# Three accumulator banks in a new order, and gate rows and key stores on GpSimd's queue

## The chip, the cores and the metric

The kernel runs on one core of one Trainium2 chip. The metric is device time in microseconds (us) of one execution, smaller is better; times of before are those of 3 runs. A traced execution has its own time, and a span: the stretch from its first to its last traced instruction.

## The reference, cut to what matters

One layer of a diffusion backbone over 512 latent tokens with 256 context tokens in front, width 2048, all in float32. Six modulation vectors come out of a gemv of the condition `c` with `w_ada`. Both token sets are normed and modulated and go through one input projection, which is split into the queries, keys and values of 8 differential heads and the low-rank parts of 8 latent heads.

```python
mod_x = silu(c) @ w_ada[l] + b_ada[l]               # 6 vectors of 2048: shift, scale, gate, twice
p = modulate(rmsnorm(x), sh1, s1) @ w_in            # and the same for the context tokens
q_da, k_da, v_da = heads(p[..., :3072])             # 8 heads of 128 each, rotary on q and k
c_q, c_kv = rmsnorm(p[..., 3072:3456]), rmsnorm(p[..., 3456:3712])
k_rope = p[..., 3712:]
w = softmax(q1 @ k1.T * s) - lam * softmax(q2 @ k2.T * s)   # differential heads: two maps a head
o_da = w @ v_da                                      # then latent heads, merge, output projection
x = x + g2 * ((silu(conv(g)) * u) @ w_down)          # gated MLP, then a final norm
```

## The kernel before, in words

Every float32 operand is split in two (`split`, L245: ScalarE casts the high part, VectorE subtracts for the low part), and a product is three matmuls (`mm3`, L281) of some 0.23 us each for 512 columns.

**Stages.** The profile's time axis has these: up to about 140 us the norm, the first modulation rows and the first five features; from 140 to 296 us the *feature stage*; from 296 to 425 us the *values*; then attention, the output projection and the MLP.

**The feature stage** (L863 to L885) makes the remaining key features of the differential heads (f = 0 to 5), the rotary key (f = 6) and three features `cq` for the latent queries. Each feature takes two weight blocks of 512 KB. A block is loaded by `wload` (L257, SP's queue, a ring of three `wr` tiles), cast by ScalarE to `wh` (L248, L268 for the rotary one) and completed by VectorE with `wl` (L249). A finished key feature goes through `keys` (L759): rotary, split into `kh` and `kl`, and `put` (L768) stores both to DRAM, 384 KB each. After each feature come `next_gemv` calls (L875, L885): three rows for f = 0 to 5, two for the others, 26 in all. One row is a load of 1024 KB into a ring of two `ada` tiles (L349) and one VectorE instruction (L352, "gate row" from here on) that leaves one column of modulation in `modx`. All of these loads and stores are issued on SP's queue, which takes them one after the other: an issue that waits (for a ring's tile, or for `kl`) holds all issues behind it. Only the three `cq` pairs are stored through GpSimd's queue. The order of the instructions in this stage is not written by hand, the framework's scheduler lays it out from the program and a model of times.

**The values** (L902 to L945) multiply all 768 tokens by the value weights in two halves of 512 columns. Each half has six accumulators, one for each 128 tokens: four lie in the two `s` tiles and two in banks of the ring `b`. After a half, its six accumulators leave PSUM by a split into `v` tiles (L248, L249), which GpSimd's queue stores (L945). The second half leaves in the order 2, 3, 4, 5, 0, 1: first the four in the `s` tiles, then the two in banks of `b`. The last splits write tiles whose earlier content must first have been stored.

**PSUM.** Four of the eight banks are the ring `b` (pool `ps_b`), handed out in turn by `b_tile` (L242). Up to the values 19 tiles have been taken from it: 8 in the first stage, one for each of 7 features, 3 for `cq`, one for a sum. So the first half of the values takes banks 3 and 0 (counted from 0), the second half banks 1 and 2. Then the pool is released (L949) and `ps_a` takes the same four banks in the order in which its tags are first asked for, L1071 to L1073: `po` (sums of weighted values), `f` (query features), two of `pt` (transposed weights). A new tile waits for the instructions that read the old tile of its bank.

**Attention's start.** The steps of attention are put into one order by the list scheduler `Flow.run` with times of its own, which doesn't know banks. TensorE's first work is the query feature of head 1 (`da_feature`, L1130) into `f`: 7 steps of three matmuls, then the first scores of head 0 (L1013) into an `s` tile, then feature steps and scores in turn. VectorE takes the row maxima of the scores (L1016), ScalarE the exponentials (L1018). `pt` and `po` come into use with the weighted values of head 0, some 40 us after attention's start.

Of the kernel before, what the change touches and what calls it, by code (L numbers as in the profile page):

```python
# [109 lines left out]
class Flow:  # L110
# [7 lines left out]
    def buf(self, make, ring=None, count=None):  # L118
        if ring:
            self.rings[ring] = count  # L120
        return Buf(ring, make)
# [99 lines left out]
def layer_kernel(ctx: ExitStack, tc: tile.TileContext, small, rope, c_row, cc_row, x_t, ctx_t, ada, ada_k,  # L221
                 w_g0, w_f, w_v, w_uqn, w_uqr, w_ukv, w_o, w_up0, w_up, w_dn, out_t):
    nc = tc.nc
    pe, ve, sc, gp = nc.tensor, nc.vector, nc.scalar, nc.gpsimd
# [8 lines left out]
    def nm(s):  # L233
        n[0] += 1
        return f"{s}{n[0]}"
# [6 lines left out]
    def b_tile(tag="b", bufs=None):  # L242
        return ps_b.tile([P, 512], F32, tag=tag, name=nm(tag), bufs=bufs or nb[0])

    def split(dst_h, dst_l, src, scale=None):  # L245

        if scale is None:
            sc.copy(dst_h, src)  # L248
            ve.tensor_tensor(dst_l, src, dst_h.bitcast(F32), op=ALU.subtract)  # L249
        else:  # L250
            sc.mul(dst_h, src, scale)
            ve.scalar_tensor_tensor(out=dst_l, in0=src, scalar=scale, in1=dst_h.bitcast(F32),
                                    op0=ALU.mult, op1=ALU.subtract)
# [19 lines left out]
    def wblock(src):  # L273
        return wsplit(wload(src))
# [25 lines left out]
    def col(name, j=0):  # L300
        o = OFF[name] + j
        return smt[:, o:o + 1]
# [8 lines left out]
    modx = cst.tile([P, 96], F32, name="modx")  # L311
# [26 lines left out]
    def rstd(out, ssq, dim, t1, t2):  # L338

        sc.activation(out, ssq, AF.Ln, bias=epst, scale=1.0 / dim)  # L340
        sc.activation(out, out, AF.Exp, scale=-0.5)
        ve.tensor_scalar(out=t1, in0=ssq, scalar1=1.0 / dim, scalar2=EPS, op0=ALU.mult, op1=ALU.add)
        ve.scalar_tensor_tensor(out=t2, in0=out, scalar=-0.5, in1=out, op0=ALU.mult, op1=ALU.mult)
        ve.tensor_tensor(t2, t2, t1, op=ALU.mult)
        ve.scalar_tensor_tensor(out=out, in0=t2, scalar=1.5, in1=out, op0=ALU.add, op1=ALU.mult)

    def gemv(pool, j, srcs, bufs=2):
        w = pool.tile([P, D], F32, tag="ada", name=nm("ada"), bufs=bufs)
        nc.sync.dma_start(w, ada[j])  # L349
        for i, (vec, dst) in enumerate(srcs):  # L350
            junk = w if i == len(srcs) - 1 else pool.tile([P, D], BF16, tag="junk", name=nm("junk"), bufs=1)
            ve.tensor_tensor_reduce(out=junk, in0=w, in1=vec, op0=ALU.mult, op1=ALU.add, scale=1.0,  # L352
                                    scalar=col("b_ada", j), accum_out=dst[:, j:j + 1])
# [10 lines left out]
    cb = st.tile([P, D], F32, name="cb")  # L364
# [83 lines left out]
    for p in range(8):  # L448
# [5 lines left out]
        def ctx_square(q=q, kts=kts, p=p):  # L454
            if p in ON_DVE:
                ve.tensor_tensor(hv(q(), kts, 1), cv(kts), cv(kts), op=ALU.mult)
            else:
# [3 lines left out]
             w=[q], hold=[cr[p // 2]])  # L461
# [34 lines left out]
    for k, (c0, c1) in enumerate(((0, T), (T, TT))):  # L496
        r, s, g = rinv[:, c0:c1], slice(c0, c1), 1 - 0.38 * k
# [233 lines left out]
    kv = tc.alloc_tile_pool(name="kv", bufs=1, reuse_waits="tile")  # L731
    kvs = tc.alloc_tile_pool(name="kvs", bufs=2, reuse_waits="tile")
    cb = kv.tile([P, D], F32, name="cb1")
# [7 lines left out]
    def next_gemv(pool, count):  # L741
        for _ in range(count):
            j = next(gv, None)
            if j is not None:
                gemv(pool, j, [(cb, modx)])

    lo, hi = slice(0, 64), slice(64, 128)

# [16 lines left out]
        split(kh[:, T:], kl[:, T:], co)  # L765
        put(dst, (kh, kl))

    def put(dst, hl, queue=nc.sync):  # L768
        for i in range(2):
            queue.dma_start(dst[i], hl[i].bitcast(F32))  # L770

# [6 lines left out]
                                    op0=ALU.mult, op1=ALU.subtract)  # L778
        return qs

    def latent_norm(tiles, squares, s, width, dim, wname, dst, queue=nc.sync):
        total = squares[0][:, :width]
        root = []

        def add():
            for q in squares[1:]:
                ve.tensor_tensor(total, total, q[:, :width], op=ALU.add)
            for c0, c1 in [(0, T)] if width == T else [(0, T), (T, width)]:
                pe.matmul(s[:, c0:c1], ones32, total[:, c0:c1], start=True, stop=True)

        def roots():
            r, t1, t2 = (kv.tile([P, TT], F32, tag=g, name=nm(g), bufs=1)[:, :width] for g in ("nr", "n1", "nq"))
            rstd(r, s[:, :width], dim, t1, t2)
            root.append(r)

        def scaled(i, t):
            ve.scalar_tensor_tensor(out=t, in0=t, scalar=col(wname, i), in1=root[0], op0=ALU.mult, op1=ALU.mult)
            hl = [kvs.tile([P, TT], F32R, tag=g, name=nm(g))[:, :width] for g in ("kh", "kl")]
            split(hl[0], hl[1], t)
            put(dst[i], hl, queue)  # L800

        return [add, roots] + [lambda i=i, t=t: scaled(i, t) for i, t in enumerate(tiles)]
# [60 lines left out]
    for f in range(7):  # L863
        lat, co = b_tile(), s_tile()[:, :T]
        if f < 6:
            feature(lat, co)
            keys(k_d[f + 2], lat, halves_sum(co))
            if f == 0:
                for part in latent_norm(ckv, sq, s_tile(), TT, KVR, "kvn", ckv_d):
                    part()  # L870
        else:
            rotary_feature(lat, co)
            lat = parts_sum(lat, kv.tile([P, T], F32, tag="qs0", name=nm("lt"), bufs=1))
            keys(kr_d, lat, parts_sum(halves_sum(co), kv.tile([P, C], F32, tag="ct", name=nm("ct"), bufs=2)))
        next_gemv(kv, 3 if f < 6 else 2)  # L875
    cq, sq = [], []
    for i in range(3):
        lat = b_tile()
        feature(lat, None)
        sq.append(kv.tile([P, TT], F32, tag=("nq", "nr", "n1")[i], name=nm("nq"), bufs=1))  # L880
        sc.square(sq[i][:, :T], lat)
        t = kv.tile([P, TT], F32, tag="lt", name=nm("cq"), bufs=3)[:, :T]
        sc.copy(t, lat)
        cq.append(t)
        next_gemv(kv, 2)  # L885
    queries = latent_norm(cq, sq, b_tile(), T, QR, "qn", cq_d, gp)
    raws, rows = [], []

# [35 lines left out]
    with tc.manual_schedule(engines={mybir.EngineType.PE, mybir.EngineType.Activation, mybir.EngineType.DVE,  # L924
# [4 lines left out]
        for half in range(2):  # L929
# [8 lines left out]
            for t in order:  # L938
                hl = []
                for _ in range(2):  # L940
                    pool, g, bufs = homes.pop(0)
# [27 lines left out]
    def block(t, *src):  # L969

        cols = sum(p.shape[1] for p in src)
        raw = fetch(t, src, cols)
        hi = buf(lambda: wp.tile([P, 1024], F32R, tag="wh", name=nm("wh"), bufs=3), "wh", 3)
        lo = buf(lambda: wp.tile([P, 1024], F32R, tag="wl", name=nm("wl"), bufs=3), "wl", 3)
        step("ACT", 0.05 + cols * 0.00088, t - 4, lambda: sc.copy(hi()[:, :cols], raw()[:, :cols]), r=[raw], w=[hi])
        step("DVE", 0.02 + cols * 0.0011, t - 2.8, lambda: ve.tensor_tensor(
            lo()[:, :cols], raw()[:, :cols], hi()[:, :cols].bitcast(F32), op=ALU.subtract), r=[raw, hi], w=[lo],
             lock=True)
        return hi, lo
# [76 lines left out]
    def weights_tile():  # L1056
        return buf(lambda: dp.tile([P, TT], F32, tag="p0", name=nm("p0"), bufs=8), "p0", 8)
# [10 lines left out]
    da.tile([P, T], F32, tag="rt", name=nm("rt"), bufs=2)  # L1068
    for _ in range(4):
        weights_tile().make()  # L1070
    b_tile("po", 1)  # L1071
    b_tile("f", 1)
    b_tile("pt", 2)  # L1073
    zeroed = [buf(lambda t=t: t) for t in klz]
    for n_, (t, b) in enumerate(zip(klz, zeroed)):
        for i, r in enumerate((hi, lo)):
# [75 lines left out]
    for h in range(NH):  # L1152
# [21 lines left out]
        if h + 1 < NH:  # L1174
# [4 lines left out]
            else:  # L1179
# [3 lines left out]
        hl = wvals[h]  # L1183
        flow.part = f"w{h}"
        weighted_values(BASE[h + 1] + 4.0, 3.05, ws, lambda kt, hl=hl: [g()[:, kt * P:(kt + 1) * P] for g in hl],
                        lambda kt, hl=hl: hl, o,
                        lambda t, o, h=h: step("SP", 0.4, t, lambda: nc.sync.dma_start(o_d[h], o()), r=[o],
                                               w=[o_ready[h]]))
# [63 lines left out]
    def head_value(t, p, kt, w, s=None):  # L1252

        out = s or buf(lambda: b_tile("f", 1), "f", 1)
        o = TT if s else 0

        def mm():
            for j in range(2):
                mm3(out()[:, o:o + 256], [g[:, kt * P:(kt + 1) * P] for g in lat["ckv"][j]],
                    [g()[:, j * 256:j * 256 + 256] for g in w], j == 0 and not s, j == 1, s is not None)  # L1260

        if kt % 3 == 0:
            mv[p, kt // 3] = [vals(g) for g in ("vh", "vl")]
        c = slice(kt % 3 * 256, kt % 3 * 256 + 256)
        step("PE", 0.73, t, mm, r=[*w, latent_open], w=[out])
        parts(t + 0.95, mv[p, kt // 3], out, lambda b: b()[:, c], lambda: out()[:, o:o + 256], None, 0.27, 0.4)
# [55 lines left out]
    for h in range(-1, NH):  # L1322
# [19 lines left out]
        for qt in range(NQT):  # L1342
# [8 lines left out]
            if i == 0 and qt == 3:  # L1351
# [4 lines left out]
                   None if kt is None else lambda t, s, kt=kt: head_value(t, p, kt, vw[p], s))  # L1356
# [37 lines left out]
    def a2k(dt=F32, pool=None):  # L1394
        return (pool or pools["apa"]).tile([P, 512], dt, tag="a2k", name=nm("a2k"))
# [14 lines left out]
    for kb in range(8):  # L1410
        t = tw + 8 * 0.9 * kb
        w = block(t, w_o[0, kb])
        for j in range(2):
            h = 2 * kb + j
            hl = [buf(lambda: a2k(F32R)), buf(lambda: a2k(F32R, pools["apb"]))]
# [29 lines left out]
    cb = wo.tile([P, D], F32, name="cb2")  # L1445
# [34 lines left out]
    for g in range(3):  # L1480
# [7 lines left out]
        for kb in range(8 if g else 0):  # L1488
            next_gemv(wo, 1)
            w = g1_first.pop(0) if g1_first else wblock(w_o[g, kb])  # L1490
# [138 lines left out]
    queue = []  # L1629
# [569 lines left out]
```

## Time and profile before

| | |
|---|---|
| median of 3 runs | 2345.67 us (2344.15 to 2346.49) |
| the traced execution | 2343.4 us |
| its span | 2341.6 us |
| granted TensorE clock, mean | 0.993 |
| busy in the span: TensorE, VectorE, ScalarE, GpSimd | 98%, 74%, 50%, 11% |

The rows of stages give the busy time of PE, PEld, DVE, ACT and POOL in that order, each with its count of instructions. Busy time of TensorE counts matmuls whose ends are modelled, so 98% says that it rarely stands still and not that each matmul runs at its best pace. A granted clock of 1.00 is 2.4 GHz. In the rows, L is a line of the kernel, "PEld" is TensorE's weight load, "SPq" and "POOLq" are the DMA issues of SyncE's and GpSimd's queues, and an arrow in brackets gives the idle time of the engine before the instruction and what ended it.

### The profile page before, as it was taken

What the parts mean: (1) busy time and instruction counts of PE and PEld (TensorE: products, weight loads), DVE (VectorE), ACT (ScalarE), POOL (GpSimd) and SP (SyncE); (2) the same over time, 40 slices, a digit from 0 to 9 for tenths busy, and PEclk for the clock granted to TensorE, in tenths of its full rate; (3) what the DMA queues carried; (4) which work ended last, traced back from release to release, by engine and by line L of the source; (5) the groups of instructions that cost most, each with busy time, mean ns of one, the idle gap of its engine ahead of it and who ended that gap; (6) DMA issues with size and microseconds to landing.
All of it is one profiled execution on the core that took longest, in us unless ns stands there. A gap on an engine that the chain in (4) does not pass through costs nothing.

```text
span 2341.6 us, 32200 instructions
## 1 busy us (share of the span) xinstructions
PE 2292.9 (98%) x12378; PEld 1960.5 (84%) x12378; DVE 1729.7 (74%) x2206; ACT 1166.3 (50%) x1777; POOL 267.7 (11%) x308
## 2 busy tenths in 40 slices
PE   6999999999999999999999999999999999999998
PEld 5788788788888888898888888888888888888887
DVE  7988876598987676597685858585858585767667
ACT  6541311477767522355454545454545454545456
POOL 0000001100123212000101010101010101010110
PEclk8999999999999999999999999999999999999999
DMA  9978989545311197234647374646464555555563
GB/s 370 368 254 293 354 321 324 176 123 164 126 35 41 55 349 279 100 102 142 144 117 165 105 172 115 159 121 153 126 145 134 137 143 144 131 149 126 154 184 105
DMA packets 124731, 404.23 MB, mean 173 GB/s; under 512 B 14337, under 2 KB 18945, under 8 KB 114081
## 3 DMA queue, kind: packets, MB, share of 16 engines
q1 hardware_dynamic: 96658, 346.92, 44.3%
q0 software_dynamic: 26768, 54.21, 12.5%
q8 instruction: 97, 1.59, 0.3%
q10 hardware_dynamic: 1152, 1.05, 0.1%
q14 instruction: 56, 0.46, 0.1%
HBM read 332.45 MB, written 69.67 MB: 172 GB/s over the span
## 4 chain that ended last, share of the span: by engine, by line
PE 84%; DVE 7%; issue 4%; DMA 3%; ACT 1%; POOL 0%; SPq 0%; DVEq 0%; ACTq 0%; POOLq 0%
PE y L1911 13%; PE b L284 9%; PE b L285 9%; PE b L286 9%; PE y L1913 7%; PE z L1911 6%; PE s L1013 4%; PE z L1913 3%; PE x L1911 3%; PE s L284 3%; PE s L285 3%; PE s L286 3%; DMA ada<-in_ada 2%; PE x L1913 2%; PE f L284 2%
## 5 line engine op out<-in xcount | busy, mean ns | idle before, releaser
L1735 DVE TENSOR_TENSOR wl<-wr,wh 128x1024 fp32r<-128x1024 f32 x144 | 176.4, 1225 | 158.9 <-ACT wh L1727 158.2
L1932 POOL DMA_DIRECT2D x_d<-xs x160 | 139.7, 1000 | 1147.5 <-ACT xs L1931 1145.6
L1727 ACT CAST wh<-wr 128x1024 fp32r<-128x1024 f32 x144 | 150.8, 1048 | 216.6 <-PE b L285 119.2
L284 PE MATMUL b<-ah,wh 128*128 128x512 f32 (+1 forms) x664 | 256.8, 387 | 0.0
L285 PE MATMUL b<-al,wh 128*128 128x512 f32 (+1 forms) x664 | 256.7, 387 | 0.0
L286 PE MATMUL b<-ah,wl 128*128 128x512 f32 (+1 forms) x664 | 255.9, 385 | 0.0
L1735 DVE TENSOR_TENSOR wl<-rb,wh 128x1024 fp32r<-128x1024 f32 x123 | 149.9, 1219 | 120.6 <-ACT wh L1727 120.6
L1735 DVE TENSOR_TENSOR wl<-ws,wh 128x1024 fp32r<-128x1024 f32 x123 | 150.3, 1222 | 110.4 <-ACT wh L1727 110.4
L1727 ACT CAST wh<-rb 128x1024 fp32r<-128x1024 f32 x123 | 129.3, 1051 | 182.7 <-PE b L285 80.1
L1911 PE MATMUL y<-a2k,wh 128*128 128x512 f32 x656 | 164.0, 392 | 0.0
L1727 ACT CAST wh<-ws 128x1024 fp32r<-128x1024 f32 x123 | 128.4, 1044 | 68.2 <-PE b L285 48.8
L286 PEld LDWEIGHTS b<-ah,wl 128*128 128x128 f32 x664 | 124.8, 188 | 25.7
L284 PEld LDWEIGHTS b<-ah,wh 128*128 128x128 f32 x664 | 125.1, 188 | 22.9
L285 PEld LDWEIGHTS b<-al,wh 128*128 128x128 f32 x664 | 125.1, 188 | 21.9
L1911 PEld LDWEIGHTS y<-a2k,wh 128*128 128x128 f32 x656 | 118.6, 189 | 21.6
L248 ACT CAST wh<-wr 128x1024 fp32r<-128x1024 f32 x51 | 53.5, 1051 | 160.6 <-DMA wr<-in_w_v 47.1
L352 DVE CUSTOM_DVE_ANT_0 ada<-ada,cb,smt 128x2048 f32<-128x2048 f32 x42 | 101.5, 2418 | 26.4 <-DMA ada<-in_ada 26.4
L1018 ACT ACTIVATE p<-s,m 128x768 f32<-128x768 f32 x96 | 86.8, 905 | 48.3 <-DVE m L1016 47.0
L1016 DVE TENSOR_REDUCE m<-s 128x1 f32<-128x768 f32 x96 | 91.0, 950 | 24.5 <-PE s L1013 24.2
L1911 PE MATMUL y<-b2k,wh 128*128 128x512 f32 x410 | 106.8, 390 | 0.0
L1931 ACT ACTIVATE xs<-b,modx 128x512 f32<-128x512 f32 x160 | 101.2, 681 | 1.7 <-DMA x_d<-xs 1.6
L1913 PEld LDWEIGHTS y<-a2k,wl 128*128 128x128 f32 x656 | 89.5, 190 | 6.4
(523 smaller groups left out, 5931.5 us busy)
## 6 DMA issues: line engine op xcount, KB each, us to landing
ada<-in_ada SPq DMA_DIRECT2D x80, 1024.0 KB, 6.8
rb<-in_w_up SPq DMA_DIRECT2D x123, 512.0 KB, 4.4
wr<-in_w_dn SPq DMA_DIRECT2D x88, 512.0 KB, 3.6
x_d<-xs POOLq DMA_DIRECT2D x160, 256.0 KB, 6.0
wr<-in_w_up SPq DMA_DIRECT2D x53, 512.0 KB, 4.2
wr<-in_w_f SPq DMA_DIRECT2D x34, 512.0 KB, 6.9
adak<-in_ada_k SPq DMA_DIRECT2D x32, 512.0 KB, 7.5
wr<-in_w_o SPq DMA_DIRECT2D x32, 512.0 KB, 6.5
```

Source lines behind the costliest of these rows:

```text
L284: pe.matmul(out, st[0], mv[0], start=start, stop=False, **kw)
L285: pe.matmul(out, st[0], mv[1], start=False, stop=False, **kw)
L286: pe.matmul(out, st[1], mv[0], start=False, stop=stop, **kw)
L352: ve.tensor_tensor_reduce(out=junk, in0=w, in1=vec, op0=ALU.mult, op1=ALU.add, scale=1.0, scalar=col("b_ada", j), accum_out=dst[:, j:j + 1])
L1013: pe.matmul(s()[:, c0:c1], a, b[:, c0:c1], start=i == 0, stop=i == len(ms) - 1)
L1016: step("DVE", 0.87, t + cost + 0.2, lambda: ve.tensor_reduce(out=m(), in_=s()[:, :TT], axis=AX.X, op=ALU.max, negate=True), r=[s], w=[m])
L1727: sc.copy(t, raw[:, k * n_:k * n_ + n_])
L1735: ve.tensor_tensor(t, raw[:, k * n_:k * n_ + n_], hi[k].bitcast(F32), op=ALU.subtract)
L1911: pe.matmul(o, w[j][0], hs[j], start=start and j == 0, stop=False, skip_group_check=True)
L1913: pe.matmul(o[:, h0], w[j][1], hs[j][:, h0], start=False, stop=j == 7, skip_group_check=True)
L1931: sc.mul(x, po, modx[:, 80 + dt:81 + dt])
L1932: gp.dma_start(x1_d[dt], x, accum_op=ALU.add)
```

## The change

Three edits. `gemv` takes a queue, and rows asked for with the pool `kv` (the 26 of the feature stage) are loaded through GpSimd's queue; the rows during the values (`load_row`, L893) and those of later stages stay on SP's. `put` and `latent_norm` have GpSimd's queue as default: that moves 24 stores of the features, 16 of keys (`k_d`), 2 of the rotary key (`kr_d`), 2 of the first queries (`q0_d`) and 4 of the latent keys and values (`ckv_d`). And attention's pool asks for `pt` first, so its banks are `pt`, `pt`, `po`, `f`.

```diff
-    def gemv(pool, j, srcs, bufs=2):
+    def gemv(pool, j, srcs, bufs=2, queue=nc.sync):
         w = pool.tile([P, D], F32, tag="ada", name=nm("ada"), bufs=bufs)
-        nc.sync.dma_start(w, ada[j])
+        queue.dma_start(w, ada[j])
...
             if j is not None:
-                gemv(pool, j, [(cb, modx)])
+                gemv(pool, j, [(cb, modx)], queue=gp if pool is kv else nc.sync)
...
-    def put(dst, hl, queue=nc.sync):
+    def put(dst, hl, queue=gp):
         for i in range(2):
             queue.dma_start(dst[i], hl[i].bitcast(F32))
...
-    def latent_norm(tiles, squares, s, width, dim, wname, dst, queue=nc.sync):
+    def latent_norm(tiles, squares, s, width, dim, wname, dst, queue=gp):
...
     for _ in range(4):
         weights_tile().make()
+    b_tile("pt", 2)
     b_tile("po", 1)
     b_tile("f", 1)
-    b_tile("pt", 2)
```

## Rows read from the trace of the kernel before

**Rows 1.** Stages: window, length, busy us of five engines, clock, DMA, GB/s.

```profile
140.00:256.00 116.00, 116.00 (x567) 98.03 (x566) 98.12 (x143) 32.12 (x49) 0.00 (x0) 1.00 0.83 296
256.00:296.00 40.00, 37.85 (x159) 30.38 (x158) 35.71 (x40) 15.49 (x23) 0.00 (x0) 0.96 0.94 349
296.00:425.00 129.00, 128.86 (x567) 106.06 (x565) 83.50 (x82) 23.47 (x29) 14.19 (x21) 1.00 0.92 320
425.00:440.00 15.00, 10.39 (x39) 8.48 (x40) 4.61 (x6) 3.60 (x6) 7.00 (x10) 0.77 0.68 258
```

**Rows 2.** TensorE's waits before and after 425 us: total, times, longest.

```profile
PE b L286 <- DVE wl L249: 2.1, 1, 2.1
...
PE f L284 <- DVE v L249: 4.7, 1, 4.7
```

**Rows 3.** TensorE in order of time where attention starts: start, us, instruction.

```profile
424.48 0.39 PE L286 MATMUL b<-wh,a4k 128*128 128x512 f32 x1
429.61 0.80 PE L284 MATMUL f<-a4k,wh 128*128 128x512 f32 x1 [4.75 <-DVE v L249]
...
433.62 0.45 PE L284 MATMUL f<-a4k,wh 128*128 128x512 f32 x1
...
436.44 0.39 PE L1013 MATMUL s<-ks,qs 128*128 128x512 f32 x1
```

**Rows 4.** VectorE in order of time at the same place.

```profile
428.87 0.69 DVE L249 TENSOR_TENSOR v<-b,n 128x512 fp32r<-128x512 f32 x1 [2.08 <-DMA v_d<-v]
431.19 0.69 DVE L249 TENSOR_TENSOR v<-b,v 128x512 fp32r<-128x512 f32 x1 [1.63 <-DMA v_d<-v]
437.32 0.96 DVE L1016 TENSOR_REDUCE m<-s 128x1 f32<-128x768 f32 x1 [5.44 <-PE s L1013]
```

**Rows 5.** TensorE in order of time at the last features' start.

```profile
256.46 0.40 PE L285 MATMUL b<-a4k,wh 128*128 128x512 f32 x1
...
258.93 0.50 PE L286 MATMUL b<-a4k,wl 128*128 128x512 f32 x1 [2.06 <-DVE wl L249]
...
262.78 0.53 PE L284 MATMUL b<-a4k,wh 128*128 128x512 f32 x1
```

**Rows 6.** VectorE in order of time before that.

```profile
224.30 2.56 DVE L249 TENSOR_TENSOR wl<-wr,wh 128x1024 fp32r<-128x1024 f32 x2
...
242.71 0.69 DVE L270 TENSOR_TENSOR wh<-wr,wh 128x512 fp32r<-128x512 f32 x1 [0.25 <-ACT wh L268]
...
251.27 2.35 DVE L352 CUSTOM_DVE_ANT_0 ada<-ada,cb,smt 128x2048 f32<-128x2048 f32 x1 [2.90 <-DMA ada<-in_ada]
...
254.79 2.33 DVE L352 CUSTOM_DVE_ANT_0 ada<-ada,cb,smt 128x2048 f32<-128x2048 f32 x1
...
257.65 1.22 DVE L249 TENSOR_TENSOR wl<-wr,wh 128x1024 fp32r<-128x1024 f32 x1
```

**Rows 7.** ScalarE at the same place.

```profile
255.02 1.05 ACT L248 CAST wh<-wr 128x1024 fp32r<-128x1024 f32 x1 [7.10 <-DMA wr<-in_w_f]
```

**Rows 8.** SP's queue in order of time, its issues with their waits inside.

```profile
224.79 8.92 SPq L349 DMA_DIRECT2D ada<-in_ada  x2
233.76 0.90 SPq L257 DMA_DIRECT2D wr<-in_w_f  x2
...
242.86 4.64 SPq L349 DMA_DIRECT2D ada<-in_ada  x2
247.56 0.91 SPq L257 DMA_DIRECT2D wr<-in_w_f  x2
```

**Rows 9.** GpSimd's queue: its first store of that stage, start and us.

```profile
322.03 0.60 POOL L770 DMA_DIRECT2D cq_d<-kh  x1 [189.26 <-ACT kh L248]
```

**Rows 10.** DMA issues of the whole span: count, KB each, median us to landing.

```profile
ada<-in_ada SPq DMA_DIRECT2D x80, 1024.0 KB, 6.8
...
q_d<-qs SPq DMA_DIRECT2D x2, 256.0 KB, 5.9
...
cq_d<-kh POOLq DMA_DIRECT2D x3, 256.0 KB, 7.1
```

## The prediction

> **What bounds the kernel now.** I read the busy times by stage first, because the page alone (TensorE busy for 98% of the span) doesn't say where TensorE stands still. In the feature stage and in the values TensorE is busy throughout and its clock is 1.00; two short stretches are different: 256 to 296 us, with 37.85 us busy of 40, and 425 to 440 us, with 10.39 of 15 and a granted clock of 0.77 [rows 1]. TensorE sets the time, then, and what the change can win lies in these two places, or is nothing. TensorE's waits say the same in one line each: 2.1 us for a `wl` of VectorE, once, and 4.7 us for a VectorE `v` split, once [rows 2]. Both waits end on VectorE, so I went on to the order of time of TensorE and VectorE there, and from VectorE to what it waited for: SP's queue.
>
> **The place at 425 us.** The last matmul of the values starts at 424.48; one takes 0.23 us, so TensorE is free at 424.71. The first matmul of `f` starts at 429.61, after a wait for VectorE [rows 3]. VectorE's split that ends just before (428.87 + 0.69 = 429.56) is the last but one of the second half; the last one runs from 431.19 to 431.88, and both waited until earlier `v` tiles were stored [rows 4]. That agrees with the count of banks: `f` is second in its pool, bank 1, which the second half's first `b` accumulator held, and that leaves fifth of six. The gap costs 429.61 - 424.71 = 4.90 us. It costs more behind it: the next nine matmuls take from 429.61 to 433.62, 4.01 us, where nine at 0.23 take 2.07 [rows 3]; that is the stretch with the lower granted clock, of which a matmul at 0.43 shows the 1.2 GHz level and one at 0.23 the 2.4 GHz level. That is 1.94 us more, 6.84 us in all.
>
> With `pt`, `pt`, `po`, `f` the tile `f` lies in bank 3. By the same count that is the first half's first `b` accumulator, which left when half of the 129 us of the values was over [rows 1], some 60 us earlier. Nothing else holds `f`: its two weight blocks are complete before the values end. So I take the gap and the slow clock away. `po` moves to bank 2, which leaves last (431.88), and `pt` to banks 0 and 1; they are wanted some 40 us later, and that time hides it.
>
> What is late next? The first scores start at 436.44 [rows 3]; they would start after 7 feature steps of three matmuls, 424.71 + 21 x 0.23 = 429.54, which is 6.90 earlier. The first row maximum started at 437.32 after VectorE had idled for 5.44 us; it can't start before the last split ends at 431.88, so it moves by 5.44 only [rows 4]. TensorE has nine feature steps more to do beside the scores, so I expect the later scores to keep most of the 6.8. Bounds 5.4 and 6.9; I take 6.6, near the upper one, since it is TensorE and not VectorE that the trace shows late there.
>
> **The place at 257 us.** Here the second part of the change counts. TensorE's matmul with `wl` starts at 258.93 where 256.46 + 0.23 = 256.69 was due: 2.24 us. Then ten matmul starts take from 258.93 to 262.78, 3.85 us for 2.30: 1.55 us of lower clock [rows 5]. Together 3.8 us. The `wl` ran at 257.65 behind two gate rows, of which the first had waited 2.90 us for its `ada` load [rows 6]; its `wh` was cast at 255.02 after 7.10 us of waiting for the weight load [rows 7]. Both loads came late from SP's queue. A pair of `ada` issues occupies it for 8.92 us (the second waits until a gate row gives its tile back) and the pair of weight loads behind comes at 233.76; the same again, 4.64 us, and weights at 247.56 [rows 8]. The tiles for these weights were free once VectorE had done with them: at 224.30 + 2.56 = 226.86 for the first pair and at 242.71 + 0.69 = 243.40 for the second [rows 6]. On their own queue the weights could go 6.9 and 4.2 us earlier.
>
> For the stall to go, the `wl` must move from 257.65 to 255.4, by 2.2 us. If VectorE keeps its order, it has to get both gate rows done earlier, and the first can move by its 2.90 us of waiting at most. It would, if its load weren't slowed: 1 MB of weights that now goes in the middle of the `ada` loads takes 3.5 us at the stage's 296 GB/s [rows 1] and would have gone before. The margin is 0.7 us, so I take 3.8 us as likely and not as sure; bounds 0 and 3.9, and below nothing too, for what follows.
>
> **What the moved issues cost.** 50 instructions go to GpSimd's queue, 26 loads and 24 stores. GpSimd was not busy from 140 to 296 us [rows 1] and a store of its took 0.60 us [rows 9]: 50 x 0.60 = 30 us of its 156, hidden by its idleness. What waits in that queue is the same as on SP's before: a store waits for `kl`, and `ada` loads stand behind it; the gate rows on VectorE wait for those, and the `wl` splits stand behind the gate rows. A load of 1 MB from GpSimd's queue is not in the trace. On SP's queue it lands after 6.8 us; stores of 256 KB land after 5.9 us from SP's and 7.1 us from GpSimd's queue [rows 10]. So a load lands between 0 and 1.2 us later; I take 0.3, the difference of the issue times (0.60 against 0.33), and count nothing for it while weights are early. SP's queue is left with weights alone in this stage and gains.
>
> The Trainium skill ("DMA: Bandwidth & Descriptors", Issuing engines are not separate DMA queues) says that issues from several engines share the same 16 DMA engines and save only the time of issuing. By that rule alone the second part is worth nothing and the sum is the 6.6 of the banks; the rows show more than issue time, a queue that waits for a tile and holds others.
>
> **The sum.** 6.6 + 3.8 = 10.4 us. The traced execution took 2343.4 us, its span 2341.6; they become 2333.0 and 2331.2. The median of the runs is 2345.67, 2.3 above the traced one; against it, 2335.3.
>
> **Rivals.**
> Only the banks pay: the weights come earlier, but the `wl` stays behind two gate rows that land no earlier, and TensorE stalls as before. For it: the 0.7 us of margin, and DMA engines that are busy for 0.94 of that stretch [rows 1]. Time 2345.67 - 6.6 = 2339.1.
> GpSimd's queue is too slow: gate rows land later, VectorE takes its instructions in order, and more `wl` splits come too late for their block. Each such stall costs what the one in the trace costs, 3.8 us. With the old stall and one new: 2342.9; two: 2346.7; three: 2350.5, and from three on the kernel is slower. For it: VectorE is busy 98 of 116 us in that stage [rows 1], so it can catch up little. Against it: only one block of the stage was late in the trace [rows 2], and the weights get earlier.
> The Trainium skill ("GPSIMD Engine Reference", Key points) says that GpSimd shares SBUF interfaces with VectorE and contends with instructions that read two SBUF inputs, as gate rows and `wl` splits do. No row here shows issues of GpSimd under them; by that rule this rival would be the likelier.
> The banks are not as I count: `f` lands in the bank that leaves last. Then it waits until 431.88 in place of 429.56, 2.3 us more; with the 3.8 of the features 2344.2. Against it: the wait in the trace fits the count.
>
> **How the numbers follow.** A measurement of this kernel can't tell less than about 0.2%, 4.7 us, from no change. Both parts pay: 0.50. Banks only: 0.25. GpSimd's queue too slow: 0.15, of which 0.07 for one new stall and 0.03 for two (no change), 0.05 for more (slower). Wrong bank: 0.07 (no change). An order of the feature stage that comes out worse when laid out anew: 0.03 (slower). Faster 0.75, same 0.17, slower 0.08. The prediction is the likeliest case, 2335.3. Range: below, the upper bounds of both parts and the spread of the runs, 2345.67 - 10.8 - 1.5 = 2333.4, rounded to 2333.0; above, the case of one new stall, 2342.9, which leaves out 0.18.
>
> **What would show it.** In the trace after, the first `f` matmul starts within 0.3 us of the last matmul of the values, no matmul there takes more than about 0.4 us, and the clock stays at 1.00; scores follow 7 steps later, and the first maximum right behind the last `v` split. In the feature stage, SP's weight issues follow the release of their tiles and TensorE has no wait of 2 us. It would be wrong if TensorE waits for a `wl` in several places or VectorE waits long for `ada`, if `f` still waits for a split, or if the time won before 440 us is lost to VectorE in attention.

## The result, and the profile after

The changed kernel takes 2350.61 us (median of 16 runs, 2348.03 to 2357.19), the kernel before 2345.47 in the same comparison: a ratio of 1.0026, 95% interval 1.0019 to 1.0034. It is 0.26% slower. Predicted were 2335.3 us and a gain of 10.4. The profiled execution took 2353.11 us, its span is 2351.3. It lies 2.5 us above the median of after, and the profiled one of before (2343.4) 2.1 us below the median of before, so the two traces differ by 9.7 us where the medians differ by 5.1.

The stages of after, to be read beside [rows 1] (length, then busy us of TensorE, its weight loads, VectorE, ScalarE and GpSimd, clock, DMA share, GB/s):

```profile
140.00:256.00 116.00, 111.72 (x532) 93.32 (x531) 90.92 (x132) 29.83 (x47) 20.21 (x37) 0.97 0.75 272
256.00:296.00 40.00, 32.29 (x126) 25.36 (x125) 31.56 (x41) 11.27 (x17) 7.01 (x13) 0.91 0.92 340
296.00:425.00 129.00, 129.00 (x569) 106.47 (x568) 90.03 (x86) 26.00 (x32) 12.74 (x19) 1.00 0.85 309
425.00:440.00 15.00, 15.00 (x68) 12.43 (x67) 3.60 (x4) 2.75 (x5) 1.54 (x3) 1.00 1.04 267
```

The place at 425 us has no gap any more. The loss is in the feature stage: from 140 to 296 us TensorE stands still for 4.28 + 7.71 = 11.99 us, where it stood still for 2.15, and the granted clock is 0.97 and 0.91 in the two windows, where it was 1.00 and 0.96.

The gap went as it was counted. TensorE and then VectorE of after at the end of the values, beside [rows 3] and [rows 4]:

```profile
439.87 0.39 PE L286 MATMUL b<-wh,a4k 128*128 128x512 f32 x1
440.10 0.39 PE L284 MATMUL f<-a4k,wh 128*128 128x512 f32 x1
...
444.86 0.39 PE L1013 MATMUL s<-ks,qs 128*128 128x512 f32 x1
```

```profile
444.42 0.69 DVE L249 TENSOR_TENSOR v<-b,n 128x512 fp32r<-128x512 f32 x1 [2.24 <-DMA v_d<-v]
446.93 0.69 DVE L249 TENSOR_TENSOR v<-b,v 128x512 fp32r<-128x512 f32 x1 [1.82 <-DMA v_d<-v]
447.54 0.95 DVE L1016 TENSOR_REDUCE m<-s 128x1 f32<-128x768 f32 x1
```

`f` starts 0.23 us behind the last matmul of the values, the scores follow seven steps later, and the first row maximum stands right behind the last split. To see what that is worth I take the distance from the last matmul of the values to the fifth row maximum of head 0: 448.69 - 424.48 = 24.21 us before, 458.05 - 439.87 = 18.18 after. The banks brought 6.03 us here, but the values end 439.87 - 424.48 = 15.39 us later.

TensorE's waits of after from 140 to 300 us, beside the first line of [rows 2], and where they stand in time:

```profile
PE b L286 <- DVE wl L249: 7.6, 2, 4.1
PE b L284 <- ACT wh L248: 2.7, 1, 2.7
PE b L852 <- DVE wh L270: 0.9, 1, 0.9
PE b L284 <- DVE ckv L816: 0.6, 1, 0.6
```

```profile
156.30 0.50 PE L284 MATMUL b<-a4k,wh 128*128 128x512 f32 x1 [2.71 <-ACT wh L248]
...
268.83 0.50 PE L286 MATMUL b<-a4k,wl 128*128 128x512 f32 x1 [4.06 <-DVE wl L249]
285.60 0.50 PE L286 MATMUL b<-a4k,wl 128*128 128x512 f32 x1 [3.52 <-DVE wl L249]
```

They add up to 11.8 us, where before had 2.1. The rest of the 15.39, some 5.7 us, is for the most part time in which TensorE counts as busy, since its idle time grew by only 11.99 - 2.15 = 9.84 us: matmuls at the lower granted clock behind such stalls (the rows show 0.50 for one, 0.39 at a clock of 1.00). The first stall shows the pattern. VectorE, ScalarE and GpSimd ahead of it:

```profile
151.27 2.35 DVE L352 CUSTOM_DVE_ANT_0 ada<-ada,cb,smt 128x2048 f32<-128x2048 f32 x1 [5.93 <-DMA ada<-in_ada]
...
154.49 0.41 DVE L816 COPY ckv<-b 128x256 f32<-128x256 f32 x1
```

```profile
154.93 0.38 ACT L815 ACTIVATE nq<-b 128x256 f32<-128x256 f32 x1 [8.33 <-DVE ckv L816]
155.21 2.93 ACT L248 CAST wh<-wr 128x1024 fp32r<-128x1024 f32 x3
```

```profile
145.56 0.72 POOL L349 DMA_DIRECT2D ada<-in_ada  x1 [14.23 <-DMA wr<-in_w_f]
```

The gate row at 151.27 waited 5.93 us for a load that GpSimd's queue issued at 145.56, after it had waited for a weight load. `ckv` stands behind it on VectorE, ScalarE's `nq` waits 8.33 us for `ckv`, the `wh` casts stand behind `nq`, and TensorE waits for `wh`. Before, SP's queue issued this load later, at 147.77, and yet nothing waited: both `ckv` stood ahead of the gate row. VectorE of before:

```profile
147.24 0.42 DVE L816 COPY ckv<-b 128x256 f32<-128x256 f32 x1
148.11 0.42 DVE L816 COPY ckv<-b 128x256 f32<-128x256 f32 x1 [0.45 <-ACT nq L815]
...
157.28 2.34 DVE L352 CUSTOM_DVE_ANT_0 ada<-ada,cb,smt 128x2048 f32<-128x2048 f32 x1
```

With its loads and stores on another queue the scheduler laid the feature stage out anew, with gate rows further ahead. VectorE's gate rows wait 26.2 us for their loads from 140 to 296 us; before it was 13.6, and 9.9 in a second trace of before.

Two theories follow. *Order*: the loss is the new order, in which work that TensorE needs stands behind gate rows whose loads aren't there. *Queue*: loads through GpSimd's queue land later, in whatever order.

### The profile page after: what moved, and what is told of

It is laid out like the page before. It is cut to its first block, busy times and chain, and to the rows that moved or that the text cites. A ratio compares the mean times of both kernels' runs of the same rounds, so it can differ in the third digit from the quotient of the medians.

```text
span 2351.3 us, 32225 instructions
## 1 busy us (share of the span) xinstructions
PE 2296.7 (98%) x12378; PEld 1962.1 (83%) x12378; DVE 1727.8 (73%) x2206; ACT 1165.2 (50%) x1777; POOL 293.7 (12%) x358
## 4 chain that ended last, share of the span: by engine, by line
PE 83%; issue 6%; DVE 6%; DMA 2%; ACT 1%; POOL 1%; SPq 0%; DVEq 0%; POOLq 0%; ACTq 0%
PE y L1911 13%; PE b L284 9%; PE b L285 9%; PE b L286 9%; PE y L1913 7%; PE z L1911 6%; PE s L1013 4%; PE z L1913 3%; PE x L1911 3%; PE s L284 3%; PE s L285 2%; PE s L286 2%; PE x L1913 2%; PE pt L1033 1%; DMA ada<-in_ada 1%
```

## The experiments

To hold an order, some kernels carry edges without a wait between neighbours of one engine, from the feature stage to the queries' norm; `ORDERS` lists, for VectorE, ScalarE and TensorE, the order that the kernel before (or after) has there.

```python
def pin(nc, tc, mark):
    for engine, order in ORDERS.items():
        made = [i for i in nc.cur_bb.bb.instructions[mark:] if i.engine == engine and "Tile" not in str(i.opcode)]
        seq = []
        for r in order.split():
            a, n = (r + "+1").split("+")[:2]
            seq += made[int(a):int(a) + int(n)]
        ...
        for x, y in zip(seq, seq[1:]):
            tc.add_manual_dep(y, x.name, mybir.DependencyInfo(mybir.DependencyClass.NoSync, mybir.DependencyReason.DATA),
                              reason="pin")
```

The orders in which SP's and GpSimd's queues issue are not held. They are laid out with each kernel, so "order" below means the order of the three engines with the issues that came out beside it. In e1 SP's queue issues its loads as in before; in e12 gate rows and weights alternate in another way.

All results first. A ratio is against the kernel before in the same comparison; the last three columns are times in the profiled execution, from the span's start.

| kernel | ratio (95%) | median us | last values matmul | fifth maximum | distance |
|---|---|---|---|---|---|
| before | | 2345.47 | 424.48 | 448.69 | 24.21 |
| before, again | | 2341.71 (one run) | 423.26 | 447.03 | 23.77 |
| after | 1.0026 (1.0019 to 1.0034) | 2350.61 | 439.87 | 458.05 | 18.18 |
| e1 banks alone | 0.9990 (0.9981 to 1.0000) | 2340.72 | 421.79 | 445.53 | 23.74 |
| e2 queues alone | 1.0060 (1.0045 to 1.0075) | 2357.85 | 436.81 | 461.80 | 24.99 |
| e3 banks, loads | 1.0036 (1.0023 to 1.0050) | 2350.37 | 438.61 | 456.05 | 17.44 |
| e4 banks, stores | 1.0002 (0.9992 to 1.0011) | 2345.25 | 431.80 | 449.91 | 18.11 |
| e5 after, old order | 0.9995 (0.9986 to 1.0004) | 2342.33 | 429.94 | 448.22 | 18.28 |
| e6 banks, new order | 1.0029 (1.0019 to 1.0039) | 2349.23 | 438.20 | 456.64 | 18.44 |
| e7 banks, `vh` late | 0.9975 (0.9961 to 0.9989) | 2337.47 | 425.87 | 443.33 | 17.46 |
| e9 e5 and a swap | 1.0002 (0.9990 to 1.0014) | 2343.01 | 431.15 | 449.31 | 18.16 |
| e10 e7 and a swap | 0.9979 (0.9968 to 0.9989) | 2338.98 | 422.23 | 439.47 | 17.24 |
| e11 e9 and `vh` late | 0.9996 (0.9988 to 1.0004) | 2342.57 | 429.25 | 446.48 | 17.23 |
| e12 e4, old order | 0.9967 (0.9956 to 0.9979) | 2335.53 | 425.65 | 443.06 | 17.41 |

**Parts alone.** e1 is the change of `b_tile` calls alone, e3 adds the loads to it (`queue=gp` in `gemv`), e4 the stores (`queue=gp` in `put` and `latent_norm`).

```diff
+    b_tile("pt", 2)
     b_tile("po", 1)
     b_tile("f", 1)
-    b_tile("pt", 2)
```

> Only the new order of the banks; loads and stores stay on SP's queue, and the orders of TensorE and VectorE are those of the kernel before. In the trace after, the distance from the last values matmul to the same softmax step of head 0 shrank by 6.0 us (the loss of 15.4 us before the last values matmul had become 9.4 us at that step). Both theories (order, queue) expect that alone here: 6 us faster than before, 2339 to 2340, the last values matmul where it was before (424 to 425 us after the span's start, within 1), no gap ahead of the first f matmul. If less than 3 us come off, what the banks win early in attention is lost again later, and part of the loss of the whole change would lie there.

> New banks; the 26 loads of gate rows through GpSimd's queue, the stores of keys and latents back on SP's. VectorE's order, laid out anew, begins like that of the whole change: gate rows stand ahead of ckv, kl and wl instructions. Theory order (gate rows moved up wait for their loads and hold the weight splits behind them): the last values matmul comes at 437 to 442 us, about 15 late as after, time 2348 to 2352. Theory queue, in the form that loads wait behind stores in GpSimd's queue: without the stores the loads are early, and the time falls to that of the banks alone, 2339 to 2342.

> New banks; the stores of keys and latents through GpSimd's queue, the gate rows' loads stay on SP's. TensorE's order is that of before, VectorE's differs in where some gate rows and weight splits stand. Theory order: few gate rows stand earlier, so most of the loss goes, 2338 to 2343. Theory queue, in the form that GpSimd's issues are what is slow: stores are not waited for by the feature stage, so 2338 to 2341 as well; it is told from the row above by that one. Over 2346 would speak against both and for the stores.

e3 is as slow as the whole change, without one moved store, so loads that wait behind stores are not the cause. e4, whose order was laid out anew too, lies above what either theory gave it; its trace has two waits for a `wl`, 6.9 us in all, though its interval overlaps that of e1. And e1 gained only 0.10%, by an interval that reaches to no change, less than half of what was expected: the gap is gone, but the distance shrank by only 0.47 us. VectorE, ScalarE and TensorE of e1:

```profile
427.99 0.69 DVE L249 TENSOR_TENSOR v<-b,n 128x512 fp32r<-128x512 f32 x1 [3.89 <-DMA v_d<-v]
430.50 0.69 DVE L249 TENSOR_TENSOR v<-b,v 128x512 fp32r<-128x512 f32 x1 [1.82 <-DMA v_d<-v]
431.11 0.95 DVE L1016 TENSOR_REDUCE m<-s 128x1 f32<-128x768 f32 x1
```

```profile
435.37 0.90 ACT L1018 ACTIVATE p<-s,m 128x768 f32<-128x768 f32 x1 [4.62 <-DMA v_d<-nq]
```

```profile
436.41 0.50 PE L1013 MATMUL s<-ks,qs 128*128 128x512 f32 x1 [4.65 <-ACT p L1018]
```

In this execution the values end at 421.79, 2.69 us earlier than in that of before, yet the last split ends at 431.19 where it ended at 431.88 [rows 4]: it waits for stores of earlier `v` tiles. The first exponential writes where `nq` lay and waits until that is stored, and the third group of score matmuls waits for the exponential. The DMA engines of e1 from 415 to 436 us, in 40 slices:

```profile
DMA  9999999999999999999999999999999999999999
GB/s 209 238 265 373 371 193 224 217 205 211 298 211 205 199 217 257 287 351 402 427 390 433 390 406 390 414 414 377 402 390 400 414 402 375 421 380 388 396 386 373
```

They are busy in every slice, but up to 424 us they move for the most part some 200 GB/s, behind that some 400. The loads that land by 425 us are those of attention's keys (`ks`, `klz`) and one block of weights, issued from 405 to 414 us. `vh` and `vl`, issued from 414.81 to 422.25, land only from 425.7 to 436.5, beside the stores, in the faster stretch. e10, in which `vh` and `vl` come later, has a slow stretch as well (221 GB/s from 415 to 420 us), so it isn't they that make it.

**The order alone, the old order, the queues alone.** e5 is the whole change with the order of before, e6 is e1 (all on SP's queue) with the order of after, e2 is the whole change with the old `b_tile` calls.

> The whole change, loads and stores on GpSimd's queue, new banks, but the instructions of VectorE, ScalarE and TensorE from the feature stage on to the queries' norm are held in the order of the kernel before (edges without a wait between neighbours of one engine). Theory order: the loss goes, the last values matmul comes at 420 to 426 us, time 2333 to 2340, that is at least what the banks alone give; 2335 if the 3.8 us of the prediction's feature stage come too. Theory queue (loads through GpSimd's queue land later or are held there, whatever the order): most of the loss stays, the last values matmul at 433 us or later, time 2345 to 2352.

> The counterpart of the pinned kernel: new banks, all loads and stores on SP's queue, but VectorE, ScalarE and TensorE from the feature stage to the queries' norm held in the order of the changed kernel (gate rows moved up). Theory order: it loses like the whole change although nothing goes through GpSimd's queue; last values matmul at 434 to 440 us, time 2346 to 2352, and on SP's queue, where the weights stand behind the loads of gate rows, perhaps more. Theory queue: without GpSimd's queue nothing is late, last values matmul at 421 to 425 us, time 2339 to 2342.

> Only the queues, the banks in the old order. In the whole change the banks brought 6.0 us by the trace (the distance from the last values matmul to the same softmax step: 24.2 us before, 18.2 after). If that holds, this kernel is 5 to 7 us slower than the whole change, 2354 to 2357. In the banks-alone kernel the same distance shrank only to 23.7, since VectorE's last splits and ScalarE's first exponential waited for the stores of the values; if such waits come here too the loss is smaller, 2 to 4 us, 2351 to 2354.

e6 decides for order: with nothing on GpSimd's queue it is 1.0029, against 0.9990 for the same kernel in the order of before, some 9 us. The last values matmul comes at 438.20, as the theory of order had it (434 to 440), and the gate rows wait 27.4 us for their loads, as after's do. TensorE's waits of e6 from 140 to 300 us are of the two kinds that after has:

```profile
PE b L286 <- DVE wl L249: 5.6, 1, 5.6
PE b L284 <- ACT wh L248: 4.3, 1, 4.3
```

From the other side, e5 takes 0.31% (7 us) off the whole change. Its time, and its last values matmul at 429.94, lie between what the two theories gave it, so order may not be all; by the ratios alone it can't be told from e1, whose interval overlaps its own. e2 shows that the banks are worth 0.34% beside moved queues, somewhat more than expected: 24.99 us of distance against 18.18.

**The values' stores.** e7 is e1 with four loads behind the twelve `v_d` stores:

```diff
-                nc.sync.dma_start(hl[i]().bitcast(F32), v_d[h // 4]...
+                (gp if h < 2 else nc.sync).dma_start(hl[i]().bitcast(F32), v_d[h // 4]...
```

> Banks alone, with one thing more: the vh and vl loads of heads 0 and 1, four times 384 KB, go through GpSimd's queue and so behind the twelve stores of the values; on SP's queue they were issued at 414 to 423 us, ahead of those stores, and are wanted at 465. Theory (what the banks win is lost to the values' stores, which queue behind loads that nobody wants yet): the stores land earlier, the last v splits end by about 427 in place of 431.2, the first exponential starts 3 to 4 us earlier than 435.4, time 2336 to 2338. Rival (the rest of the gain is lost elsewhere, or the DMA engines are bound by the sum of the bytes whatever their order): 2340 to 2342, as the banks alone. If the loads come too late for the weighted values, TensorE waits for vh at 465 and the time rises.

0.9975: 3.5 us less than e1 by the ratios, whose intervals just overlap. The time came in as expected, but in the traced execution the gain is not where I put it: the last split ends at 432.72 and not by 427, since the values end at 425.87 this time, and the first exponential starts at 434.76, 0.6 us earlier than in e1 and not 3 to 4. Only the distance falls from 23.74 to 17.46 us and the first exponential waits for VectorE, not for a store. e10, where the values end at 422.23, shows more, but its traced execution is the fastest of its twelve (2333.59 us; the median is 2338.98), and its key loads too were issued 4 us earlier than in e1 (401.18 against 405.38). VectorE and ScalarE of e10:

```profile
424.68 0.69 DVE L249 TENSOR_TENSOR v<-b,n 128x512 fp32r<-128x512 f32 x1 [0.15 <-DMA v_d<-v]
426.04 0.69 DVE L249 TENSOR_TENSOR v<-b,v 128x512 fp32r<-128x512 f32 x1 [0.67 <-ACT v L248]
428.10 0.96 DVE L1016 TENSOR_REDUCE m<-s 128x1 f32<-128x768 f32 x1 [1.37 <-PE s L1013]
```

```profile
429.14 0.91 ACT L1018 ACTIVATE p<-s,m 128x768 f32<-128x768 f32 x1 [2.28 <-DVE m L1016]
```

The splits wait for next to no store, and the first maximum waits for TensorE again. How much of that is due to `vh` and `vl` isn't shown.

**The kernel before once more.**

> The kernel before, unchanged, profiled a second time, to see whether its wait of 2.1 us for a wl at 257 us is there in each execution: the kernel with the banks alone has the same orders of VectorE and TensorE and showed none. If the wait is a matter of when loads land in one execution, it is elsewhere, larger, smaller or missing here, and the last values matmul lies up to 3 us from 424.5; if it belongs to the kernel it stands at 257 us with 2 us again.

TensorE in this trace:

```profile
270.56 0.50 PE L286 MATMUL b<-a4k,wl 128*128 128x512 f32 x1 [1.27 <-DVE wl L249]
```

The only wait for a `wl` was 1.27 us, and it stood at 270 us, at a later block; e1, with the same orders, had none. It is not a fixed cost of one place; as expected there, it goes with when loads land in an execution.

**One `wl` ahead of one gate row.** e9 is e5, e10 is e7 with the order of before, and e11 is e9 with `vh` and `vl` late; each has one swap in `ORDERS` of VectorE (102 is the gate row, 103 the `wl`):

```diff
-        "89 84 90 85 91 86 92 100 93 99 101 94+2 102 96 103 97 104 98 114+2 105+2 108+2 107 110 113 111 116 "
+        "89 84 90 85 91 86 92 100 93 99 101 94+2 103 102 96+2 104 98 114+2 105+2 108+2 107 110 113 111 116 "
```

> The pinned kernel (both queues, new banks, order of before) with one swap: the wl of the last key block, which stood behind a gate row that waited 3.67 us for its load and so held TensorE for 4.92 us at 259 us, goes ahead of that gate row. Its wh was cast by 253.1, so it can run at 256.2, before TensorE wants it at 259.05. Theory order (each loss of the feature stage is a wl behind a gate row whose load isn't there): the wait goes, the last values matmul comes 4 to 6 us earlier than 429.94, at 424 to 426, time 2337 to 2340 against 2342.3. Theory queue (loads and weights that come side by side are late as a whole): another wait takes its place, the last values matmul stays at 428 or later, time 2341 to 2343.

> The kernel with the loads of vh and vl behind the values' stores, all else on SP's queue, with the order of before held and the same swap. On SP's queue the wh of that block was cast at 255.0 only, so the wl can start at 256.1 and the wait of 1.3 to 2.1 us at 257 shrinks to under 1. Theory order: 2335 to 2337 against 2337.5, hardly to be told from it. If the swap does nothing, the same time.

> The whole change with the order of before held, the swap, and the vh and vl loads behind the values' stores. If the order was all that was wrong with moving the queues, this is at least as good as its counterpart on SP's queue: 2334 to 2337. If loads through GpSimd's queue cost landing time whatever the order, it is 2 to 5 us slower than its counterpart, 2338 to 2342.

In e5 the one stall left was this, VectorE and then TensorE:

```profile
259.82 2.35 DVE L352 CUSTOM_DVE_ANT_0 ada<-ada,cb,smt 128x2048 f32<-128x2048 f32 x1 [3.67 <-DMA ada<-in_ada]
...
262.70 1.22 DVE L249 TENSOR_TENSOR wl<-wr,wh 128x1024 fp32r<-128x1024 f32 x1
```

```profile
263.97 0.79 PE L286 MATMUL b<-a4k,wl 128*128 128x512 f32 x1 [4.92 <-DVE wl L249]
```

In e9 that `wl` runs at 256.97 and the stall is gone. VectorE, ScalarE and TensorE of e9 show what took its place:

```profile
256.97 1.21 DVE L249 TENSOR_TENSOR wl<-wr,wh 128x1024 fp32r<-128x1024 f32 x1
260.57 2.35 DVE L352 CUSTOM_DVE_ANT_0 ada<-ada,cb,smt 128x2048 f32<-128x2048 f32 x1 [2.39 <-DMA ada<-in_ada]
```

```profile
271.88 0.40 ACT L858 COPY ct<-ct 64x256 f32<-64x256 f32 x1 [5.37 <-DVE ct L756]
...
272.73 1.05 ACT L248 CAST wh<-wr 128x1024 fp32r<-128x1024 f32 x1
```

```profile
273.82 0.55 PE L284 MATMUL b<-a4k,wh 128*128 128x512 f32 x1 [3.08 <-ACT wh L248]
276.33 0.80 PE L286 MATMUL b<-a4k,wl 128*128 128x512 f32 x1 [1.53 <-DVE wl L249]
```

The gate row still waits; two more follow at 265.92 and 268.56, then `ct`, for which ScalarE waits 5.37 us with the next `wh` cast behind it. The stall has moved back by 12 us and lost 0.3 us (3.08 + 1.53 against 4.92). Here the theory of order alone fails: e9 isn't faster than e5, and e11 (0.9996) is slower than its counterpart on SP's queue, e10 (0.9979), with the same order on the three engines (the intervals overlap by a hair). e10 gains nothing on e7.

**Loads or stores.** e12 is e4 with the order of before.

> New banks, the order of before held, only the stores of keys and latents through GpSimd's queue; the gate rows' loads and the weights stay on SP's. With the order held, the whole change cost 1 to 4 us against its counterpart on SP's queue; this tells loads from stores. If it is the loads (gate rows and weights are under way side by side, and both land later), the gate rows here wait for their loads as in the banks-alone kernel, 9 to 12 us in all from 140 to 296 us in place of 15 to 20, and the time is that of the banks alone, 2339 to 2341. If it is the stores, 2342 to 2344 as in the whole change with the order held.

0.9967 is the lowest of all, 7.7 us less than before (the intervals of e7 and e10 overlap it), and neither expectation came in. Against e4, the same kernel in the order that the scheduler gave it, it is 0.35% less, which shows the price of the order once more. The stores on GpSimd's queue cost nothing; beside e1 they gain 0.23% (the intervals just miss each other). What costs are the loads: e5, which has them as well, is 0.28% slower than e12. The sign that I had named for it doesn't show: the gate rows wait 17.7 us here and not 9 to 12, between e1 (11.4) and e5 (20.4), although e12 is the fastest. Both differences are measured, but their way through the trace isn't known, and SP's order of issue changed with them.

The traces of e1 and e12 also show what the distance depends on. SP's last load ahead of attention, GpSimd's store of `nq` and the time that this store took to land, in e1 and then in e12:

```profile
422.25 0.33 SPq L1106 DMA_DIRECT2D vl<-v_d  x1
424.83 0.75 POOL L945 DMA_DIRECT2D v_d<-nq  x1
v_d<-nq POOLq DMA_DIRECT2D x1, 256.0 KB, 10.4
```

```profile
422.23 0.41 SPq L1106 DMA_DIRECT2D vl<-v_d  x1
428.68 0.75 POOL L945 DMA_DIRECT2D v_d<-nq  x1
v_d<-nq POOLq DMA_DIRECT2D x1, 256.0 KB, 5.7
```

The loads were issued at the same time. In e12 the values ended 3.86 us later, their stores came that much further behind the loads, and the store of `nq` landed at 434.4 us where it landed at 435.2 in e1. So values that end earlier gain little here while the loads don't come earlier too: in e1 the last `vl` was issued 0.46 us behind the last values matmul. In the ten traces with `vl` issued 3.1 to 4.5 us ahead of it, that store landed in 4.0 to 7.1 us.

## Why the prediction was wrong

By ratios that are each known to some 0.1%: the banks -0.10% (e1); the stores on GpSimd's queue, order held, -0.23% (e12 against e1); the loads on it, order held, +0.28% (e5 against e12); the new order +0.31% (after against e5). That sums to +0.26%, as it must, since each step starts where the last one ended. Along another path the shares differ: the banks -0.10% (e1), the new order +0.39% (e6 against e1), the moved loads and stores in that order -0.03% (after against e6), which is nothing. On either path it is the new order that makes the loss.

**The step that failed** is the one behind the 3.8 us of the features: "If VectorE keeps its order, it has to get both gate rows done earlier". It doesn't keep it. A new order had a chance of 0.03, and the text before says that the scheduler lays this stage out from a model of times: two `dma_start` calls moved to another queue are reason enough to expect another order. Held in the old order the same change is 0.9995, so the new order turned no change into a loss; and e6, with nothing moved to GpSimd's queue, loses 0.29% by that order. In place of a stall of 2.1 us that goes, after has three of 4.1, 3.5 and 2.7 us.

With the order kept the 3.8 us didn't come either. In e5 the first of the two gate rows ran without a wait, but the second waited 3.67 us for its load, and the same `wl` held TensorE for 4.92 us where it had been 2.06.

**The cost of the moved loads** was put too low. "I take 0.3 ... and count nothing for it while weights are early." By e5 against e12 the loads cost 0.28%, some 6.5 us, in the old order. Longer landing is not shown to be the reason. With the order held, a load of gate rows landed in 7.2, 7.6 and 7.1 us (medians of e5, e9, e11 from 140 to 296 us), against 6.8, 6.9 and 6.6 in e1, e7 and e10, and the weights in 8.0, 7.4 and 7.9 against 7.0, 6.9 and 6.9. But the loads of e12, all on SP's queue, took 7.3 us and it is fast, and those of e2 and e3, on GpSimd's queue in the new order, took 6.0 and 6.1. That weights which SP's queue no longer holds back travel beside the gate rows' loads, what the text called "its load weren't slowed", is only argued. How the loads cost what they cost stays open; the chain of waits in e9 shows one way.

**The rule of the Trainium skill** ("DMA: Bandwidth & Descriptors", Issuing engines are not separate DMA queues), that a DMA goes to the same 16 engines whoever issues it, agrees with the traces: from 140 to 296 us the one queue of before took 85.4% of the engines' time for 48.14 MB, the two of after 62.1% for 35.08 and 17.0% for 9.92, 1.7 to 1.8% for a MB each time. "Worth nothing" didn't follow from it: who issues sets when, and in what order, all else is laid out. The other rule of the Trainium skill ("GPSIMD Engine Reference", Key points), on interfaces shared with VectorE, shows nothing here: a gate row took 2.347 us before and 2.348 after (means), a `wl` 1.220 and 1.215, beside GpSimd's issues.

**The banks** were right in mechanism; their 6.6 us were mis-sized for a kernel that loses nothing ahead of them. The gap goes as counted, and 6.0 us come where the values end late (after). In e1, where they end early (421.79), the last split still ends at 431.2 and the exponential waits for a store, and by the ratio 2.3 us are left. So the sum 6.6 + 3.8 was not a sum. The prediction read that limit, "it can't start before the last split ends at 431.88", kept it fixed for the banks and forgot it when it added the features: both terms are paid through the same stores. That the limit is the loads queued on the DMA engines ahead of those stores fits the traces of e1, e12 and e10 (the store of `nq` landed in 10.4, 5.7 and 3.5 us); no run moved those loads alone and earlier.

**The rivals.** "GpSimd's queue is too slow" had the right picture, gate rows that hold `wl` splits, but not the cause: e6 has such stalls with all loads on SP's queue. Its price of 3.8 us a stall counts the slow clock behind it; the waits of after alone are 4.06, 3.52 and 2.71 us, and with the clock they are most of the 15.39 us by which the values end later. That its time for three new stalls, 2350.5, is 0.1 us off the measured median is luck. The rival that came true, an order "that comes out worse when laid out anew", had no price. "Only the banks pay" is not it, nor "the banks are not as I count". The stall of before at 257 us, on which the 3.8 us rested, was not there in its second trace.

## What to carry to other kernels

Where a scheduler lays out the order, a moved DMA can be a new order: compare the instruction order before any cost is worked out, and hold the old order to see the move by itself. Shares that are read off step by step depend on the path of the steps; a second path tells how much. Before two gains are added, ask whether the next limit behind them is the same; here the stores of the values were behind both. A stall seen in one execution is worth a second trace before a gain is built on it.

## What the runs showed of the hardware

DMA engines that show busy in every slice moved some 200 GB/s while attention's key loads and a block of weights landed, and 400 while `vh`, `vl`, more weights and the values' stores did, in one stretch of 21 us (e1). A store of 256 KB took 3.5 us to land where the loads ahead of it were through (e10), 5.7 us where the last load had been issued 6.5 us ahead (e12), and 10.4 us where it was 2.6 us (e1). Moving 1.5 MB of loads behind such stores gave some 0.15% (e7 against e1), by intervals that overlap. What was not expected is the stores of keys and latents: on GpSimd's queue, order held, they are worth 0.23% (e12 against e1). The two traces differ by 2.9 us, of which 2.5 are there at the fifth maximum; why the ratios differ by some 5 us stays open.
